# GpSimd's side work in an attention loop: four short pieces a quarter, and second pieces in units 3 to 24

## The chip, the cores and the metric

The kernel runs on one core of a Trainium2 chip. The core has five engines that each take their own instructions in order: TensorE (PE in the profile, with its weight loads as PEld), VectorE (DVE), ScalarE (ACT), GpSimd (POOL) and SyncE (SP, which here only issues transfers). They wait for each other by semaphores. The metric is the device time of one execution in microseconds (us), the median of several runs; lower is better.

## What is computed

One layer of a diffusion backbone on 1024 latent tokens of width 1024, with 256 context tokens, all in float32. The part that the change touches is the windowed attention:

```
hx = modulate(rmsnorm(x), sh1, sc1)
q, k, v, u, b, c, g_attn, g_conv = split(hx @ w_in)
for each block of 128 queries, each head:          # 8 blocks, 16 heads in 4 groups of 4
    s = q_block @ [k in the window of 384 keys | k_ctx of 256 keys].T / 8
    p = softmax([s masked | sink of the head])      # the sink only adds to the denominator
    o = p[:, :-1] @ [v in the window | v_ctx]
x = x + g1 * merge(o, conv(u, b, c), g_attn, g_conv) @ w_out
x = x + g2 * expert_choice_moe(modulate(rmsnorm(x), sh2, sc2))   # 16 experts of 128 tokens
return rmsnorm(x) * final_norm_g
```

A product of float32 matrices is made of three products of a high part and a low part (hi x hi, hi x lo, lo x hi). Large products behind the attention use a scheme of seven block products in place of eight, which wants sums and differences of the blocks of its operands beforehand.

## The kernel before

The stages are: modulation and the projections of q, k, v; the attention loop (about 250 to 600 us of the trace); the block products of the convolution branch and of the projections; the routing; the experts.

**The attention loop** (lines 784 to 802) has 32 units, one for each group g of four heads and block i of 128 queries. Unit n does this, in up to six steps s:

- `cur.turn(s)`: TensorE transposes the probabilities of one chunk of 128 keys for four heads (line 670, into psT), ScalarE casts them to the high part `th` (line 673), VectorE subtracts for the low part `tl` (line 674).
- `nxt.scores(s)` for s below 4: the scores of one head of unit n+2, two units ahead: TensorE's four products (lines 646 and 647), VectorE's masked maximum (line 649), ScalarE's exponential with its sum (line 653).
- At s = 3, `nxt.normalise()`: VectorE adds the sink's part to the sums (lines 660 and 662) and takes the reciprocal (line 663), then GpSimd multiplies the four heads' probabilities by it (line 665, four instructions). The transposes of unit n+2 need these.
- `pour(1)`: one step of the gate projection on TensorE (lines 40 to 44, three products into psF). These steps fill TensorE's time; there are 256 of them in all, and what is left of them is done behind the loop.
- `next(pool_left)` at some steps: one piece of GpSimd's side work, below.
- `cur.values(s - 1)`: the products with v (lines 682 and 683, into psB), at the last chunk ScalarE's copy and VectorE's sum (lines 687 and 688) and the store of the unit's result to `od`.

**GpSimd's side work** is a generator, `pool_work`, cut into pieces by its `yield`s:

- Three rows of the modulation (`mod_row`), each of eight pieces k = 0 to 7, with a piece ahead of the first row that only loads. A piece multiplies a loaded tile of 128 x 1024 by a column (line 477), adds it to `acc` (line 481; not for k = 0) and issues the load of the tile two pieces later (line 468, two tiles `w` in turn). At k = 1 it issues the loads for k = 2 and k = 3 together.
- `x_sums` for four quarters: sums and differences of the blocks of the layer's normalised input, in three parts of three, three and four instructions on 128 x 512 (line 696), in two tiles `w`. Behind the last part ScalarE casts each tile to `whi` (line 716), VectorE subtracts for `wlo` (line 717), and SyncE stores both to `xd`. The next quarter's first two parts write the same two tiles, so they wait for line 717.
- `o_sums` for two of four slices of the attention's output, heads of groups 0 and 2: the loads from `od` (line 738), four subtractions (line 725), then ScalarE's cast (line 728), VectorE's subtraction (line 729) and the stores to `sums`.

**What sets the order.** GpSimd's order in the loop is that of the code, since line 782 sets it by hand; it takes each instruction as soon as the one ahead is done and its waits are over. The other engines' orders come from the framework's scheduler, which places instructions by its own model; on chip they are fixed. Their order moves a little when the pieces move. A piece is taken at s = 4 of each unit, and at s = 1 where the condition of line 797 says so (second pieces). An assertion keeps the loads from `od` behind unit 24, as unit 23 is the last one of group 2.

Of the kernel before, what the change touches and what calls it, by code (L numbers as in the profile page):

```python
# [27 lines left out]
def hybrid_layer(ctx, tc, x, c, cx, c_ctx, w_mod, b_mod, norm1_g, w_in, attn_sink, conv_w,  # L28
# [320 lines left out]
    def pour(n):  # L349
        for _ in range(n):  # L350
            next(fill, None)
# [340 lines left out]
    def x_sums(ks):  # L692

        def part(hl, kh, th):
            return X[hl, kh, th].bitcast(F32)[:, ks]
        add, sub = ((lambda o, a, b, op=op: nc.gpsimd.tensor_tensor(out=o, in0=a, in1=b, op=op)) for op in (OP.add, OP.subtract))
        r = [w_tile(), w_tile()]
        t1, t2, t3, t4 = r[0][:, 0:512], r[0][:, 512:1024], r[1][:, 0:512], r[1][:, 512:1024]
        sub(t1, part(0, 0, 1), part(0, 0, 0))
        sub(t2, part(1, 0, 1), part(1, 0, 0))  # L700
        add(t1, t1, t2)
        yield
        sub(t3, part(0, 1, 1), part(0, 0, 1))
        sub(t4, part(1, 1, 1), part(1, 0, 1))
        add(t3, t3, t4)
        yield
        sub(t2, part(0, 1, 1), t1)
        add(t2, t2, part(1, 1, 1))
        sub(t4, part(0, 1, 0), t2)
        add(t4, t4, part(1, 1, 0))  # L710
        yield
        for n in range(2):
            hi = stage.tile([128, 2, 512], FR, name="whi", bufs=2)
            lo = stage.tile([128, 2, 512], FR, name="wlo", bufs=2)
            rv = r[n].rearrange("p (a b) -> p a b", a=2)
            nc.scalar.copy(out=hi, in_=rv)
            nc.vector.tensor_tensor(out=lo, in0=rv, in1=hi.bitcast(F32), op=OP.subtract)
            for hl, v in ((0, hi), (1, lo)):
                nc.sync.dma_start(out=xd[n * 2:n * 2 + 2, hl, :, ks].rearrange("n p f -> p n f"), in_=v.bitcast(F32))
# [23 lines left out]
    def w_tile():  # L743
        return osp.tile([128, 1024], F32, name="w", bufs=2)

    def pool_work():
        for n in range(1, 4):
            yield from mod_row(n, w_tile, lambda: osp.tile([128, 1024], F32, name="acc"), n < 3)
        for ks in range(4):
            yield from x_sums(ks)  # L750
        for ks in range(2):

            yield from o_sums(ks)
# [13 lines left out]
    piece = [0]  # L767
# [16 lines left out]
    for n in range(len(order)):  # L784
        cur = units.pop(0)
        nxt = Unit(*order[n + 2]) if n + 2 < len(order) else None
        units.append(nxt)
        nch = len(cur.chunks)
        for s in range(nch + 1):
            if s < nch:  # L790
                cur.turn(s)
            if nxt and s < 4:
                nxt.scores(s)
                if s == 3:
                    nxt.normalise()
            pour(1)
            if s == 4 or s == 1 and n % 3 == 0:
                piece[0] += 1
                assert piece[0] < 37 or n > 24
                next(pool_left, None)  # L800
            if s > 0:
                cur.values(s - 1)
# [240 lines left out]
    for m in range(4):  # L1043
        n = 3 * m + 3
# [872 lines left out]
```

## Time and profile before

| | us |
|---|---|
| three runs, median | 1795.31 |
| three runs, lowest and highest | 1794.01 and 1802.44 |
| the profiled execution | 1792.85 |
| its span, first to last instruction | 1791.0 |
| TensorE busy | 1711.4 (96%) |
| VectorE busy | 1412.4 (79%) |
| ScalarE busy | 1005.0 (56%) |
| GpSimd busy | 483.3 (27%) |

TensorE is busy in nearly all of the span, so a row of the profile matters where it ends one of TensorE's waits. GpSimd's 27% is an average over stages: it is at work most of the time from about 280 to 600 us, and hardly at all in many other stretches. Where an engine is followed in order of time, the bracket at a row's end is the idle time of that engine just before, and what ended it.

### The profile page before, as it was taken

What the parts mean: (1) busy time and instruction counts of PE and PEld (TensorE: products, weight loads), DVE (VectorE), ACT (ScalarE), POOL (GpSimd) and SP (SyncE); (2) the same over time, 40 slices, a digit from 0 to 9 for tenths busy, and PEclk for the clock granted to TensorE, in tenths of its full rate; (3) what the DMA queues carried; (4) which work ended last, traced back from release to release, by engine and by line L of the source; (5) the groups of instructions that cost most, each with busy time, mean ns of one, the idle gap of its engine ahead of it and who ended that gap; (6) DMA issues with size and microseconds to landing.
All of it is one profiled execution on the core that took longest, in us unless ns stands there. A gap on an engine that the chain in (4) does not pass through costs nothing.

```text
span 1791.0 us, 24156 instructions
## 1 busy us (share of the span) xinstructions
PE 1711.4 (96%) x8421; PEld 1377.7 (77%) x8421; DVE 1412.4 (79%) x2052; ACT 1005.0 (56%) x1448; POOL 483.3 (27%) x374
## 2 busy tenths in 40 slices
PE   8999999999999999999898999949999999999997
PEld 5777887888877787778676877837888888888874
DVE  6867568877778358766877775679999999999996
ACT  6642157667766323232434343327878878777874
POOL 0034027778678100000000003340042233224001
PEclk8999999999999999999999999969999999999999
DMA  9465364555345853333848354689999999999755
GB/s 349 134 200 187 115 238 141 181 164 165 101 131 178 311 172 119 110 115 106 305 132 293 105 213 181 247 319 335 368 398 384 398 396 382 395 397 397 292 200 200
DMA packets 210613, 427.75 MB, mean 239 GB/s; under 512 B 17512, under 2 KB 106920, under 8 KB 207420
## 3 DMA queue, kind: packets, MB, share of 16 engines
q1 hardware_dynamic: 176348, 359.30, 54.9%
q0 software_dynamic: 12544, 46.47, 8.5%
q10 hardware_dynamic: 21600, 20.45, 3.2%
q8 instruction: 66, 1.08, 0.2%
q14 instruction: 55, 0.45, 0.1%
HBM read 349.60 MB, written 76.56 MB: 238 GB/s over the span
## 4 chain that ended last, share of the span: by engine, by line
PE 82%; DVE 9%; DMA 3%; POOL 2%; issue 2%; ACT 2%; SPq 0%; POOLq 0%; ACTq 0%; DVEq 0%
PE psA L1722 20%; PE w L855 9%; PE psB L1722 5%; PE psF L1722 5%; PE psT L855 5%; PE psA L1288 4%; PE psT L670 3%; PE psA L402 2%; PE psF L855 2%; PE psA L400 2%; PE psA L401 2%; PE psF L40 2%; PE psF L44 2%; PE psF L42 2%; PE psB L683 2%
## 5 line engine op out<-in xcount | busy, mean ns | idle before, releaser
L1722 PE MATMUL psA<-part,xeh 128*128 128x512 f32 x1024 | 281.8, 392 | 0.5 <-ACT xeh L1710 0.5
L1722 PEld LDWEIGHTS psA<-part,xeh 128*128 128x128 f32 x1024 | 191.3, 188 | 39.9 <-ACT xeh L1710 1.0
L1757 POOL DMA_INDIRECT md<-ye,idxs x15 | 106.7, 7116 | 213.1 <-DVE ye L1754 213.1
L1722 PE MATMUL psA<-part,xel 128*128 128x512 f32 x512 | 163.2, 390 | 0.0
L1580 DVE TENSOR_TENSOR part<-er,part 128x1024 fp32r<-128x1024 f32 x118 | 138.4, 1219 | 5.4 <-ACT part L1578 2.0
L1578 ACT CAST part<-er 128x1024 fp32r<-128x1024 f32 x118 | 123.7, 1056 | 32.9 <-PE psA L1722 19.9
L649 DVE CUSTOM_DVE_ANT_0 p<-psA,msk,nsink 128x640 f32<-128x640 f32 (+1 forms) x128 | 107.7, 843 | 27.3 <-PE psA L647 25.7
L1410 POOL MEMSET onesb<- 128x128 bf16 x1 | 0.2, 204 | 464.2 <-issue 464.2
L674 DVE TENSOR_TENSOR tl<-psT,th 128x512 fp32r<-128x512 f32 x152 | 103.5, 685 | 21.8 <-ACT th L673 20.4
L665 POOL TENSOR_SCALAR p<-p,l 128x640 f32<-128x640 f32 (+1 forms) x128 | 101.6, 809 | 58.0 <-DVE l L663 14.7
L653 ACT ACTIVATE p<-p,nm 128x640 f32<-128x640 f32 (+1 forms) x128 | 103.0, 805 | 21.6 <-DVE nm L649 20.8
L867 ACT CAST whi<-raw 128x1024 fp32r<-128x1024 f32 x40 | 42.0, 1050 | 130.2 <-DVE raw L898 81.7
L673 ACT CAST th<-psT 128x512 fp32r<-128x512 f32 x152 | 88.0, 584 | 48.0 <-PE psT L670 47.0
L1722 PEld LDWEIGHTS psA<-part,xel 128*128 128x128 f32 x512 | 96.2, 188 | 20.5 <-DVE xel L1711 0.3
L1580 DVE TENSOR_TENSOR part<-mh,part 128x1024 fp32r<-128x1024 f32 x88 | 105.1, 1219 | 5.1 <-ACT part L1578 2.4
L1580 DVE TENSOR_TENSOR part<-ml,part 128x1024 fp32r<-128x1024 f32 x88 | 105.3, 1219 | 4.4 <-ACT part L1578 1.6
L1578 ACT CAST part<-ml 128x1024 fp32r<-128x1024 f32 x88 | 92.3, 1053 | 25.9 <-PE psA L1722 17.5
L1578 ACT CAST part<-mh 128x1024 fp32r<-128x1024 f32 x88 | 92.2, 1053 | 25.1 <-PE psA L1722 16.5
L1580 DVE TENSOR_TENSOR part<-mp,part 128x1024 fp32r<-128x1024 f32 x85 | 100.8, 1219 | 6.5 <-ACT part L1578 3.6
L1578 ACT CAST part<-mp 128x1024 fp32r<-128x1024 f32 x88 | 92.0, 1053 | 24.3 <-PE psA L1722 15.9
L1722 PE MATMUL psB<-part,hhh 128*128 128x512 f32 x256 | 98.6, 396 | 0.2 <-ACT hhh L1710 0.2
L670 PE MATMUL psT<-identr,p 128*128 128x128 f32 x608 | 94.2, 274 | 3.1 <-POOL p L665 2.9
(496 smaller groups left out, 4558.7 us busy)
## 6 DMA issues: line engine op xcount, KB each, us to landing
raw<-in_w_in_dram SPq DMA_DIRECT2D x49, 512.0 KB, 3.7
er<-in_w_exp_down_dram SPq DMA_DIRECT2D x47, 512.0 KB, 9.3
er<-in_w_exp_up_dram SPq DMA_DIRECT2D x38, 512.0 KB, 5.4
mp<-in_w_exp_gate_dram SPq DMA_DIRECT2D x36, 512.0 KB, 8.7
mh<-in_w_exp_up_dram SPq DMA_DIRECT2D x33, 512.0 KB, 5.7
ml<-in_w_exp_up_dram SPq DMA_DIRECT2D x33, 512.0 KB, 6.2
er<-in_w_exp_gate_dram SPq DMA_DIRECT2D x32, 512.0 KB, 8.0
mh<-in_w_exp_gate_dram SPq DMA_DIRECT2D x29, 512.0 KB, 7.7
```

The lines of the kernel that those rows point to most:

```text
L649: nc.vector.tensor_tensor_reduce(out=p, in0=sp[:, 512 - n:768], in1=msk.rearrange("p a b -> p (a b)")[:, mo * 128:mo * 128 + n + L], op0=O ...
L653: nc.scalar.activation(out=p, in_=p, func=AF.Exp, scale=-1.0, bias=self.nm4[:, h:h + 1], accum_out=self.l4[:, h:h + 1])
L665: nc.gpsimd.tensor_scalar(self.pr[h], self.pr[h], l4[:, h:h + 1], 1.0, op0=OP.mult, op1=OP.mult)
L670: nc.tensor.transpose(pt[:, h * 128:(h + 1) * 128], self.pr[h][:, ci * 128:(ci + 1) * 128], ident)
L673: nc.scalar.copy(out=th, in_=pt)
L674: nc.vector.tensor_tensor(out=tl, in0=pt, in1=th.bitcast(F32), op=OP.subtract)
L855: nc.tensor.matmul(ps_, lhsT=w[a][:, o + k], rhs=xs[b][:, k], start=(first and k + a + b == 0), stop=(k == 3 and a == 1), skip_group_check ...
L1288: nc.tensor.matmul(pa[:, s], lhsT=a[t // 2][k // 4][:, k % 4, ts], rhs=w[k][:, s], start=(j == 0 and a is mh and w is woh), stop=(j == NK ...
L1578: nc.scalar.copy(out=hi, in_=raw)
L1580: eng.tensor_tensor(out=lo, in0=raw, in1=hi.bitcast(F32), op=OP.subtract)
L1722: nc.tensor.matmul(outs[s], lhsT=lh[:, k], rhs=wt[:, s * 512:s * 512 + 512], start=(k == 0 and n == 0), stop=(k == NK - 1 and n == 2))
L1757: nc.gpsimd.indirect_dma_start(out=md, out_offset=bass.IndirectOffsetOnAxis(ap=idxs[:, e:e + 1], axis=0), in_=ye, in_offset=None, compute_ ...
```

## The change

Two places of the loop's side work change. In `x_sums` a `yield` is put between the two halves of the third part, so a quarter has four parts, of three, three, two and two instructions. The condition for second pieces, which was "at s = 1 in every third unit", becomes "at s = 1 in two of three units, from unit 3 to unit 24".

```diff
         sub(t2, part(0, 1, 1), t1)
         add(t2, t2, part(1, 1, 1))
+        yield
         sub(t4, part(0, 1, 0), t2)
         add(t4, t4, part(1, 1, 0))
         yield
...
-            if s == 4 or s == 1 and n % 3 == 0:
+            if s == 4 or s == 1 and n % 3 != 2 and 2 < n < 25:
                 piece[0] += 1
-                assert piece[0] < 37 or n > 24
+                assert piece[0] < 42 or n > 24
                 next(pool_left, None)
```

The pieces to be done go from 42 to 46 (the last of each count has nothing of GpSimd's in it). Second pieces stood in units 0, 3, 6 and so on to 30, eleven in all; now there are fifteen, in units 3, 4, 6, 7 and so on to 24, so units 0 to 2 and 25 to 31 have one piece each. Lines behind 708 move down by one in the changed kernel.

GpSimd's queue around units 3 and 4, first as it is, from the second piece of unit 3 on; the names with l_ are the reciprocals of one unit, so each row of line 665 is the normalise of one unit (5, then 6):

```order
L477 TENSOR_SCALAR w<-w,sf 128x1024
L481 TENSOR_TENSOR acc<-w,acc 128x1024
L468 DMA w<-in_w_mod_dram 128x1024
L665 TENSOR_SCALAR p<-p,l_2679 128x640 x4
L477 TENSOR_SCALAR w<-w,sf 128x1024
L481 TENSOR_TENSOR acc<-w,acc 128x1024
L468 DMA w<-in_w_mod_dram 128x1024
L665 TENSOR_SCALAR p<-p,l_2810 128x640 x4
```

The same place in the changed kernel, GpSimd's queue from the second piece of unit 3 (k = 2 of the first row) to the normalise of unit 6:

```order
L477 TENSOR_SCALAR w<-w,sf 128x1024
L481 TENSOR_TENSOR acc<-w,acc 128x1024
L468 DMA w<-in_w_mod_dram 128x1024
L665 TENSOR_SCALAR p<-p,l_2675 128x640 x4
L477 TENSOR_SCALAR w<-w,sf 128x1024
L481 TENSOR_TENSOR acc<-w,acc 128x1024
L468 DMA w<-in_w_mod_dram 128x1024
L477 TENSOR_SCALAR w<-w,sf 128x1024
L481 TENSOR_TENSOR acc<-w,acc 128x1024
L468 DMA w<-in_w_mod_dram 128x1024
L665 TENSOR_SCALAR p<-p,l_2806 128x640 x4
```

Between the normalises of units 5 and 6 there are two pieces in place of one. The piece just ahead of these rows is k = 1 in the changed kernel, which issues the load for the piece at their head; before it was k = 2.

GpSimd's queue around units 24 to 26, before: the normalise of unit 26, the four instructions that end the third quarter, the normalise of unit 27, the first part of the fourth quarter, the normalise of unit 28.

```order
L665 TENSOR_SCALAR p<-p,l_5448 128x640 x4
L696 TENSOR_TENSOR w<-x_754,w 128x512
L696 TENSOR_TENSOR w<-w,x_755 128x512
L696 TENSOR_TENSOR w<-x_518,w 128x512
L696 TENSOR_TENSOR w<-w,x_519 128x512
L665 TENSOR_SCALAR p<-p,l_5564 128x640 x4
L696 TENSOR_TENSOR w<-x_698,x_306 128x512
L696 TENSOR_TENSOR w<-x_699,x_307 128x512
L696 TENSOR_TENSOR w<-w 128x512
L665 TENSOR_SCALAR p<-p,l_5708 128x640 x4
```

The same place in the changed kernel, GpSimd's queue from the normalise of unit 26 to the first loads of `o_sums`:

```order
L665 TENSOR_SCALAR p<-p,l_5472 128x640 x4
L696 TENSOR_TENSOR w<-x_754,w 128x512
L696 TENSOR_TENSOR w<-w,x_755 128x512
L665 TENSOR_SCALAR p<-p,l_5586 128x640 x4
L696 TENSOR_TENSOR w<-x_518,w 128x512
L696 TENSOR_TENSOR w<-w,x_519 128x512
L665 TENSOR_SCALAR p<-p,l_5715 128x640 x4
L739 DMA acc<-od 128x1024
L739 DMA w<-od 128x1024
```

Ahead of the normalise of unit 27 there are two instructions in place of four, and the fourth quarter is over ahead of the normalise of unit 28. In both kernels the two parts just ahead of unit 26's normalise are the first two parts of a quarter, of the third before and of the fourth now.

ScalarE's queue in the last two units, before, up to the gate's last copies; line 728 is the cast of the attention's sums, 673 that of the probabilities:

```order
L673 CAST th<-psT 128x512 x3
L728 CAST whi<-acc 128x1024
L338 COPY gs<-psF 128x512
L673 CAST th<-psT 128x512 x2
L687 COPY ot<-psB 64x512
L673 CAST th<-psT 128x512 x2
L728 CAST whi<-acc 128x1024
L673 CAST th<-psT 128x512 x2
L338 COPY gs<-psF 128x512
L687 COPY ot<-psB 64x512
```

ScalarE's queue in the same two units of the changed kernel, where line 729 is that cast:

```order
L673 CAST th<-psT 128x512 x3
L729 CAST whi<-acc 128x1024
L338 COPY gs<-psF 128x512
L673 CAST th<-psT 128x512 x2
L214 CAST whi<-raw 128x1024
L687 COPY ot<-psB 64x512
L673 CAST th<-psT 128x512 x4
L338 COPY gs<-psF 128x512
L687 COPY ot<-psB 64x512
```

The cast in unit 30 is now the second one (the first stands in unit 28), and none is left in unit 31. In TensorE's queue two groups of gate products into psF (six products) now stand between the last value product and the first gate products into psB; before, the products into psB stood right behind it.

## Rows read from the trace of the kernel before

**Rows 1.** TensorE's waits, 250 to 605 us: us in total, times, longest

```profile
PE psB L683 <- DVE tl L674: 6.2, 9, 1.0
PE psT L670 <- POOL p L665: 2.9, 3, 1.9
PE psB L682 <- ACT th L673: 2.5, 2, 1.9
PE psB L40 <- DVE ot L688: 1.4, 1, 1.4
PE psB L682 <- DVE ot L688: 1.1, 1, 1.1
```

**Rows 2.** Stretches: us, busy of PE, PEld, DVE, ACT, POOL, clock, DMA

```profile
278.00:420.00 142.00, 136.86 (x791) 115.57 (x790) 113.05 (x222) 94.96 (x205) 110.97 (x108) 1.00 0.53 167
...
520.00:545.00 25.00, 22.01 (x117) 18.11 (x116) 19.13 (x36) 15.78 (x34) 23.03 (x20) 0.93 0.55 197
...
592.00:605.00 13.00, 8.96 (x29) 6.03 (x28) 4.43 (x5) 4.13 (x6) 5.72 (x4) 0.74 0.58 199
```

**Rows 3.** GpSimd in order of time, units 4 to 7: start, us, instruction, idle before

```profile
281.11 3.13 POOL L665 TENSOR_SCALAR p<-p,l 128x640 f32<-128x640 f32 x4 [1.36 <-DVE l L663]
284.22 1.13 POOL L477 TENSOR_SCALAR w<-w,sf 128x1024 f32<-128x1024 f32 x1
...
293.31 3.11 POOL L665 TENSOR_SCALAR p<-p,l 128x640 f32<-128x640 f32 x4
...
297.60 2.40 POOL L481 TENSOR_TENSOR acc<-w,acc 128x1024 f32<-128x1024 f32 x1
300.29 0.60 POOL L468 DMA_DIRECT2D w<-in_w_mod_dram  x1 [0.30 <-POOL acc L481]
...
312.10 2.69 POOL L665 TENSOR_SCALAR p<-p,l 128x512 f32<-128x512 f32 x4 [3.40 <-DVE l L663]
```

**Rows 4.** TensorE in order of time, first transposes of units 5 and 6

```profile
300.68 0.50 PE L683 MATMUL psB<-tl,v2t 128*128 128x512 f32 x1 [0.85 <-DVE tl L674]
301.02 0.60 PE L670 MATMUL psT<-identr,p 128*128 128x128 f32 x4
...
312.01 0.60 PE L670 MATMUL psT<-identr,p 128*128 128x128 f32 x4
```

**Rows 5.** VectorE in order of time, two instructions with two tiles read

```profile
297.78 2.24 DVE L660 TENSOR_TENSOR es<-sink,nm 128x4 f32<-128x4 f32 x1
...
493.16 1.22 DVE L717 TENSOR_TENSOR wlo<-w,whi 128x1024 fp32r<-128x1024 f32 x1
```

**Rows 6.** GpSimd's groups of instructions: times, busy us, mean ns, idle before

```profile
L696 POOL TENSOR_TENSOR w<-x,x 128x512 f32<-128x512 f32 x16 | 20.3, 1289 | 14.9 <-DVE wlo L717 14.9
```

**Rows 7.** Line 468, GpSimd's loads of the modulation's weights

```profile
DMA to landing us min/median/max: 3.8/4.8/10.5
```

**Rows 8.** GpSimd in order of time, normalises of units 23 and 26

```profile
493.20 3.76 POOL L665 TENSOR_SCALAR p<-p,l 128x512 f32<-128x512 f32 x4
...
520.13 2.55 POOL L696 TENSOR_TENSOR w<-x,x 128x512 f32<-128x512 f32 x2 [7.15 <-DVE wlo L717]
...
529.36 3.12 POOL L665 TENSOR_SCALAR p<-p,l 128x640 f32<-128x640 f32 x4
```

**Rows 9.** TensorE in order of time, transposes of units 26 and 27

```profile
530.21 0.48 PE L670 MATMUL psT<-identr,p 128*128 128x128 f32 x1 [1.93 <-POOL p L665]
...
542.93 0.33 PE L670 MATMUL psT<-identr,p 128*128 128x128 f32 x1 [0.72 <-POOL p L665]
```

**Rows 10.** ScalarE in order of time, its two casts of sums that waited

```profile
557.32 1.05 ACT L716 CAST whi<-w 128x1024 fp32r<-128x1024 f32 x1 [2.76 <-POOL w L696]
...
594.47 1.05 ACT L728 CAST whi<-acc 128x1024 fp32r<-128x1024 f32 x1 [3.62 <-POOL acc L725]
```

**Rows 11.** TensorE in order of time, the last unit's end

```profile
596.05 0.50 PE L682 MATMUL psB<-th,v2t 128*128 128x512 f32 x1 [1.92 <-ACT th L673]
...
600.89 0.79 PE L40 MATMUL psB<-x,whi 128*128 128x512 f32 x1 [1.39 <-DVE ot L688]
```

## The prediction

> **What bounds the kernel now.** I read the profile from the engine that is never idle for long. TensorE is busy nearly throughout, so the change can only move the time by the moments of the attention loop in which TensorE waits or runs at its lower clock. The first view is therefore who TensorE waited for from 250 to 605 us [rows 1]: five rows, 6.2 + 2.9 + 2.5 + 1.4 + 1.1 = 14.1 us, and only 2.9 us of it names GpSimd directly. The second view says where: 142 - 136.86 = 5.1 us between 278 and 420, 25 - 22.01 = 3.0 us between 520 and 545, and 13 - 8.96 = 4.0 us between 592 and 605, where the granted clock is 0.74 as well [rows 2]. The clock has two levels, 1.2 and 2.4 GHz; a mean of 0.74 over 13 us costs 13 x 0.26 = 3.4 us. No more than about 20 us are at stake, 1% of the kernel, and nothing behind 605 us is touched by the change.
>
> Then I followed each of these waits to its cause. GpSimd works strictly in its written order: normalise four heads of unit n+2, a piece, perhaps a second piece, normalise unit n+3. One normalise is 3.12 us, a long piece is a multiply of 1.13, an add of 2.40 and the issue of a load of 0.60, with the gaps 4.5 us [rows 3]. At 312.10 it has waited 3.40 us for VectorE's reciprocal (line 663), so with one piece a unit it is ahead [rows 3]; its normalise of unit 5 ends at 296.4, and the transposes that need it stand at 301.02, 4.6 us later [rows 3, 4].
>
> **Three waits of TensorE hang on GpSimd indirectly.** (a) Early: VectorE's tiny sum of line 660 took 2.24 us from 297.78 on, and ended with GpSimd's add of 297.60 to 300.00; the next subtraction came late and TensorE stood 0.85 us [rows 3 to 5]. (b) Units 26 and 27: GpSimd stood 7.15 us until the splitting of the previous quarter's sums freed their buffer, normalised unit 26 only from 529.36 on, and TensorE waited 1.93 us; unit 27 then cost 0.72 us [rows 8, 9]. (c) ScalarE's cast of a sum stood 2.76 us for GpSimd at 557 and 3.62 us at 594, with the casts of the probabilities queued behind it; TensorE's 1.92 us at 596 and 1.39 us at 601 follow the second [rows 10, 11].
>
> **The change, part by part.** GpSimd's work is the same: the same multiplies, adds, subtractions and loads. What moves is when.
>
> *Unit 27.* Ahead of its normalise stood four subtractions and additions of 1.29 us [rows 6]; now two stand there. It comes 2 x 1.3 = 2.6 us earlier, more than the 0.72 us by which it was late: gain 0.7 us. Unit 26 keeps its order (the first two parts of a quarter, behind a buffer wait that ends at the same place of ScalarE's and VectorE's order), so its 1.93 us and the clock of 0.93 in that window [rows 2] stay: 0.
>
> *Units 28 and 29.* The fourth quarter is finished with unit 25's piece, two units earlier than now, so ScalarE's 2.76 us wait goes. Of TensorE's waits it took 1.1 us (line 682 behind VectorE's line 688) and 2.5 - 1.92 = 0.6 us (line 682 behind line 673) [rows 1, 10, 11]: gain 1.7 us. What is late next is the first cast of the attention sums, which ScalarE now reaches in unit 28; GpSimd's four subtractions stand one unit ahead of it, and I charge 0.4 us for it.
>
> *The end.* The second cast of the attention sums moves from unit 31's place to unit 30's, and the loads for its subtractions from behind the last normalise to ahead of it; the last casts of the probabilities have nothing of GpSimd's ahead of them. That removes 4.0 us of idle time and, if TensorE keeps its pace, the 3.4 us of the low clock [rows 2]. Two groups of gate products now stand between the last value product and the switch to the other bank, which covers the 1.39 us [rows 11]; the first of them needs ScalarE's copy of the bank, for which I charge 0.4 us.
>
> Sum of the gains: 0.7 + 1.7 + 4.0 + 3.4 = 9.8, less 0.8 charged: 9.0 us.
>
> *The early units, lateness.* Now the cost. The second piece comes in units 3 and 4, 6 and 7 and so on. In unit 2 GpSimd ends the normalise of unit 4 at 284.2, then the piece that adds for the first time and issues two loads (1.13 + 2.40 + 2 x 0.6 + gaps 0.4 = 5.1 us, to 289.3), and the next piece, straight behind it, needs the first of these two loads: issued at 288.1, landed 4.8 us later in the median (3.8 to 10.5) [rows 7], so it starts at 292.9 and ends at 297.4. Queued behind this wait is the normalise of unit 5, to 300.5, against transposes at 301.02: 0.5 us to spare in place of 4.6. Two pieces more, to 309.5, and the normalise of unit 6, to 312.6, against 312.01 + 0.35 for its fourth transpose [rows 4]: 0.3 us late. From there GpSimd needs 3 x 3.12 + 5 x 4.5 = 31.9 us for three units that take 312.10 - 281.11 = 31.0 us [rows 3], but each of the two row changes has a piece without an add, 3.4 us shorter, so it catches up by unit 10. Loss 0.3 us; with the landing of 10.5 us it would be 6.0, with 3.8 none. I take 0.3, since the median is the nearest.
>
> *The early units, collisions.* Case (a) becomes likelier, because GpSimd is at work when lines 660 and 662 come. Between 278 and 420 TensorE lost 5.1 us, with five second pieces in the stretch (units 3, 6, 9, 12, 15); now there are nine (3, 4, 6, 7, 9, 10, 12, 13, 15). By second pieces the loss is 5.1 x 9/5 = 9.2, 4.1 us more; by the number of long adds, which is unchanged, it is 0 more. I take the middle, 2.0. The rule for it is in the Trainium skill, SBUF — State Buffer, section "Who interferes with whom": a VectorE instruction with two inputs in SBUF contends with a GpSimd instruction that reads SBUF, and whichever issues first holds the read side for the whole instruction. The trace agrees: line 660 reads two SBUF tiles and ended with the add. It speaks against this change in both directions: GpSimd's normalise at 493.20 took 3.76 us for four heads of 512, against 2.69 at 312.10, while VectorE's line 717 ran [rows 3, 5, 8].
>
> *The middle.* The second quarter's first two parts now both stand ahead of the normalise of unit 21, behind the same buffer wait as in (b), but one unit earlier against the transposes: 0. Ahead of unit 24 one more pair of 2.6 us stands, which the 2.6 us shorter stretch ahead of unit 25 gives back: 0 to 1 us, taken as 0.
>
> Net: 9.0 - 0.3 - 2.0 = 6.7 us gained. The profiled execution took 1792.85 us with a span of 1791.0, 2.5 us under the median of 1795.31; the difference is carried over: 1795.3 - 6.7 = **1788.6 us** (profiled execution 1786.2).
>
> **Rivals.** *The dense stretch tips over (slower).* From unit 5 to 16 GpSimd runs at its limit. If in each of these 12 units two of its instructions are stretched by 3.76 - 2.69 = 1.07 us [rows 3, 8], it needs 12 x 2.14 + 4 x 0.9 = 29.3 us more than there are; the spare 4.6 and the two short pieces, 6.8, leave 17.9 us of waiting, with 4.1 for collisions: 17.9 + 4.1 - 9.0 = 13 us slower, 1808. It decides from about 1.1 us a unit on (12 x 1.1 + 3.6 - 11.4 + 4.1 = 9.5). For it: the demand of 31.9 against 31.0. Against it: the normalises at 281, 293 and 529 show none of this stretch [rows 3, 8].
>
> *Every unit collides.* If GpSimd is in an add whenever line 660 or 662 comes, each of the 13 units from 4 to 16 pays what 300.68 paid, 13 x 0.85 = 11.1 in place of 5.1: 6 more instead of 2.0, net 2.7 gained, 1792.6. For it: GpSimd never waits there any more. Against: adds fill under half of its time.
>
> *The end doesn't close.* ScalarE waits for the sums in unit 30 as it did in unit 31, or the low clock comes anyway: 7.4 - 0.4 us fall away, 1795.6, no change. For it: those subtractions stand behind the normalise of unit 31, close ahead of the cast. Against: nothing but the cast's own 1 us stands behind it, and ScalarE had idle moments around it.
>
> *Unit 26 is helped too.* If GpSimd is a little later and the buffer is free when it arrives, the 1.93 us and 25 x 0.07 = 1.75 us of clock go as well: 1785.
>
> **How the numbers follow.** Forecast 0.54; end doesn't close 0.15; every unit collides 0.17; unit 26 too 0.08; tips over 0.06. The range reaches from 1782 (all gains of 9.8 and unit 26's 3.7) to 1797 (the end open, or the long landing, with the upper price of collisions); it leaves out the tipping and some of the spread of runs. A measurement of this kernel tells about 0.5% (9 us) from no change. Faster by over that needs nearly all the gains: a quarter of the forecast's chance and most of unit 26's, and some for costs that I set too high: 0.25. Slower by over that: the tipping, 0.07. Within: 0.68.
>
> **What would show it.** After: ScalarE's waits for GpSimd at lines 717 and 729 gone or under 1 us; no low clock around 595; TensorE's wait for GpSimd in unit 27 gone, in unit 26 still there; units 5 and 6 normalised within 1 us of their transposes, and TensorE's loss between 278 and 420 near 7 us. The forecast is wrong if that loss is over 12 us, or if the stretch from 590 on still loses 4 us.

## The result and the profile after

The changed kernel takes 1817.15 us in the median (1816.61 to 1817.78) beside 1798.07 us for the kernel before on the same chip: ratio 1.0115, 95% interval 1.0094 to 1.0136. It is slower by some 20 us, where 6.7 us of gain were forecast. The profiled execution took 1816.61 us with a span of 1814.4, 23.8 us over the one of before.

Set side by side by the same instruction of TensorE, the two traces part early. Of the 608 transposes of line 670 the first comes 1.2 us earlier than before, the 100th (at 301 us) 0.7 us earlier, the 200th 5.0 us later, the 300th 12.7, the 400th (472 before, 489 now) 17.2. From there to the 480th half a microsecond is added. Unit 26 adds 2.6 (the 500th is 20.3 us late), units 27 to 29 give back 3.6 (the 540th is 16.7 late), and the end takes as much again: the first block product behind the attention (631 before) is 20.5 us late. So the early units, and what follows them up to the 400th transpose, cost some 18 us, unit 26 nearly 3, and what lies behind it, which was to give 9, gives nothing. The last 3 us are a net sum: 1 us is regained between 880 and 1060 us and 4 us are lost behind 1200, where nothing was changed; no cause of them was looked for.

TensorE's waits from 250 to 650 us, after (us in total, times, longest), answering [rows 1]:

```profile
PE psB L683 <- DVE tl L674: 14.1, 8, 3.8
PE psB L682 <- DVE ot L688: 4.9, 2, 2.8
PE psT L670 <- POOL p L665: 4.1, 3, 3.5
PE psF L40 <- ACT gs L338: 2.8, 2, 2.6
```

The first row has grown from 6.2 to 14.1 us: TensorE waits for VectorE's residue of the probabilities (the low part `tl` of line 674). For GpSimd it waits 3.5 us at unit 26 and hardly anywhere else. The stretches, after (us, busy of PE, PEld, DVE, ACT, POOL, granted clock, DMA), answering [rows 2]:

```profile
278.00:420.00 142.00, 129.01 (x712) 108.34 (x711) 111.54 (x198) 86.36 (x186) 117.68 (x109) 0.95 0.53 166
420.00:520.00 100.00, 97.56 (x554) 82.94 (x553) 78.94 (x157) 68.75 (x145) 74.44 (x67) 0.98 0.41 129
...
545.00:570.00 25.00, 21.08 (x109) 17.75 (x109) 14.71 (x29) 12.68 (x26) 18.67 (x19) 0.86 0.26 78
570.00:592.00 22.00, 18.82 (x105) 15.22 (x103) 18.37 (x33) 14.65 (x29) 14.90 (x15) 1.00 0.61 215
592.00:605.00 13.00, 12.19 (x62) 10.33 (x63) 7.45 (x15) 7.63 (x18) 4.29 (x6) 0.87 0.46 144
605.00:625.00 20.00, 16.95 (x78) 12.95 (x77) 8.60 (x12) 8.21 (x13) 4.39 (x3) 0.91 0.43 143
```

Between 278 and 420 TensorE idles 142 - 129.01 = 13.0 us (5.1 before), and the clock of 0.95 costs at most 142 x 0.05 = 7.1 us (nothing before). From 420 to 520 it idles 2.4 us (0.3 before) and the clock costs 2.0. The increases add up to 7.9 + 7.1 + 2.1 + 2.0 = 19.1 us, a little more than the 18.4 us between the first transpose and the 400th, since some 1 us of the low clock fell into idle time (0.85 from 310 to 314, below).

**Where VectorE was.** VectorE and GpSimd in order of time, after (start, us, instruction):

```profile
295.97 3.39 DVE L660 TENSOR_TENSOR es<-sink,nm 128x4 f32<-128x4 f32 x1
...
306.89 5.68 DVE L215 TENSOR_TENSOR wlo<-raw,whi 128x1024 fp32r<-128x1024 f32 x1 [0.26 <-ACT whi L214]
...
374.06 5.40 DVE L215 TENSOR_TENSOR wlo<-raw,whi 128x1024 fp32r<-128x1024 f32 x1
```

```profile
306.65 0.59 POOL L468 DMA_DIRECT2D w<-in_w_mod_dram  x1 [0.30 <-DVE tl L674]
307.29 3.12 POOL L665 TENSOR_SCALAR p<-p,l 128x640 f32<-128x640 f32 x4
310.39 1.11 POOL L477 TENSOR_SCALAR w<-w,sf 128x1024 f32<-128x1024 f32 x1
311.58 3.21 POOL L481 TENSOR_TENSOR acc<-w,acc 128x1024 f32<-128x1024 f32 x1
```

An instruction is called held here when it stands in the trace far longer than it takes by itself. Line 215, the subtraction that splits the gate's weights, takes 1.2 us undisturbed; in the kernel before its longest up to 450 us was 1.90. Here it takes 5.68 us. GpSimd runs five instructions on end meanwhile, a normalise of four heads and a row piece's multiply; the add behind them has to wait for that multiply, and between 311.50 and 311.58 GpSimd stands still. The subtraction ends at 312.57, 1.07 us after that pause began. At 374 it is the same: the multiply ends at 378.39, the subtraction at 379.46. The sum of four columns at 295.97 ends at 299.36, where the multiply of 298.24 ends. TensorE's waits for the residue that follow are 2.00 us (to 300.01), 3.81 (to 313.90) and 3.51 (to 380.93). Behind the 3.81 us the granted clock falls (stretches of the kernel after, same columns as above):

```profile
310.00:314.00 4.00, 0.19 (x2) 0.10 (x1) 4.00 (x5) 0.72 (x3) 3.92 (x3) 0.85 1.04 402
314.00:319.60 5.60, 5.60 (x17) 4.54 (x18) 3.55 (x7) 1.93 (x5) 5.09 (x7) 0.50 0.50 168
```

After a stretch in which it had stood nearly all of 4 us, TensorE works on at 0.50, which is 1.2 GHz, to 319.6. The clock is 0.50 as well from 381.1 to 384.4, behind the 3.51 us, and from 411.9 to 415.1, behind a wait of 1.81 us; behind the 2.00 us at 300.01 it stays at 1.00.

**Where the end went.** ScalarE in order of time, and SyncE's queue, after:

```profile
591.10 1.04 ACT L214 CAST whi<-raw 128x1024 fp32r<-128x1024 f32 x1 [2.82 <-DMA sums<-whi]
...
613.74 1.04 ACT L214 CAST whi<-raw 128x1024 fp32r<-128x1024 f32 x1 [4.26 <-DMA sums<-whi]
```

```profile
586.32 0.36 SPq L735 DMA_DIRECT2D sums<-w  x1
586.77 1.46 SPq L735 DMA_DIRECT2D sums<-whi  x1
```

The waits of ScalarE for GpSimd of [rows 10] are gone, as forecast. But the cast of the gate's weights now needs a `whi` buffer (there are two, shared by lines 214, 717 and 729) that the sum's cast of 582.65 has just filled, and the store that frees it stands in SyncE's queue behind the store of the other sum, from `w`. That one waits for GpSimd's last subtraction (`SPq L735 <- POOL w L726`, 11.0 us in two waits). TensorE's waits of 2.61 us at 592.81 and 2.79 us at 616.25 follow.

**Unit 26.** GpSimd and TensorE in order of time, after, answering [rows 8, 9]:

```profile
547.18 4.72 POOL L665 TENSOR_SCALAR p<-p,l 128x640 f32<-128x640 f32 x4
```

```profile
549.64 0.48 PE L670 MATMUL psT<-identr,p 128*128 128x128 f32 x1 [3.53 <-POOL p L665]
```

The normalise of unit 26 is still behind the wait for the buffer, and now takes 4.72 us in place of 3.12: its first head lasts to 549.58, since line 215 took its turn in the midst of it (547.71, 1.21 us). The wait is 3.53 us in place of 1.93, and the clock from 545 to 570 is 0.86.

### The profile page after: what moved, and what is told of

The parts are those of the page before. It is cut to its first block, busy times and chain, and to the rows that moved or that the text cites. A ratio compares the mean times of both kernels' runs of the same rounds, so it can differ in the third digit from the quotient of the medians.

```text
span 1814.4 us, 24158 instructions
## 1 busy us (share of the span) xinstructions
PE 1724.6 (95%) x8421; PEld 1391.0 (77%) x8421; DVE 1419.5 (78%) x2052; ACT 1004.5 (55%) x1448; POOL 484.1 (27%) x374
## 3 DMA queue, kind: packets, MB, share of 16 engines
q8 instruction: 66, 1.08, 0.2%
## 4 chain that ended last, share of the span: by engine, by line
PE 56%; DVE 6%; DMA 2%; issue 1%; ACT 1%; POOL 0%; SPq 0%; POOLq 0%; ACTq 0%; DVEq 0%
PE psA L1723 19%; PE w L856 9%; PE psB L1723 5%; PE psF L1723 5%; PE psT L856 4%; PE psA L1289 4%; PE psF L856 2%; PE psT L1708 2%; PE psB L856 1%; DMA x<-yd 1%; DVE rsc L1595 1%; PE part L1482 1%; DVE x L1029 1%; DVE q L934 1%; DVE mp L941 0%
## 5 line engine op out<-in xcount | busy, mean ns | idle before, releaser
L1723 PEld LDWEIGHTS psA<-part,xel 128*128 128x128 f32 x512 | 96.5, 189 | 20.5 <-DVE xel L1712 0.3
```

What stands on the lines that cost most here:

```text
L1723: nc.tensor.matmul(outs[s], lhsT=lh[:, k], rhs=wt[:, s * 512:s * 512 + 512], start=(k == 0 and n == 0), stop=(k == NK - 1 and n == 2))
```

## The experiments

Theory S (a string of GpSimd's instructions without a pause holds VectorE; from e5 on, as theory P, that VectorE gets in only at GpSimd's pauses) and theory Q (the store in SyncE's queue) stand against rival L (GpSimd comes too late with its normalises) and a loss from the fourth short piece. Where an edit adds a line to the normalise, line numbers behind it are 1 to 3 higher.

**e1_early_old**, which units carry the early loss:

```
-if s == 4 or s == 1 and n % 3 != 2 and 2 < n < 25:
+if s == 4 or s == 1 and (n % 3 == 0 if n < 16 or n > 24 else n % 3 != 2):
```

> The changed kernel, with second pieces as before up to unit 15 and after unit 24 (every third unit) and the new rule only in units 16 to 24; the four short pieces a quarter stay. Theory S (the loss is made where GpSimd's pieces stand close together in units 3 to 15, by VectorE instructions that cannot start while GpSimd's instructions follow each other without a pause): the 13.0 us that TensorE idles between 278 and 420 go back to 5 to 6, the granted clock there to 1.00, and the time is that of the kernel before plus the 3 us that the end costs: ratio 1.000 to 1.003, about 1800 us. Rival L (the loss comes from the shorter pieces or from the order after unit 16): the ratio stays at 1.008 or more, 1812 us or more.

Measured: ratio 1.0073 (1.0049 to 1.0097). Between 278 and 420 the loss is gone: TensorE is busy 137.49 of 142 us at a clock of 1.00, and the 300th transposes 1.6 us earlier than before. The time missed the expectation of 1.000 to 1.003: three pieces fewer are done by unit 24, and the sums come late again; ScalarE, in order of time:

```profile
499.50 1.04 ACT L717 CAST whi<-w 128x1024 fp32r<-128x1024 f32 x1 [5.28 <-POOL w L696]
...
607.67 1.05 ACT L729 CAST whi<-acc 128x1024 fp32r<-128x1024 f32 x1 [7.70 <-POOL acc L726]
```

The early loss belongs to the second pieces of units 3 to 15. The pieces that they bring forward are needed at the end.

**e2_rule_only**, the kernel before with the new rule alone:

```
-if s == 4 or s == 1 and n % 3 == 0:
+if s == 4 or s == 1 and n % 3 != 2 and 2 < n < 22:
```

> The kernel before with the new rule for second pieces alone (two of three units, from the 3rd to the 21st, 43 pieces), and three pieces a quarter as before. Theory S: the early loss is all there, TensorE idles 11 to 14 us between 278 and 420 with VectorE blocked for over 3 us at least three times; the end is reached with the sums two or three units earlier than before. Ratio 1.008 to 1.012, 1812 to 1819 us. Rival (the fourth short piece makes the loss): ratio within 1.003.

Measured: ratio 1.0113 (1.0075 to 1.0150). Line 215 takes 5.69 us at 307.57 and 5.40 at 374.75, and TensorE's waits between 278 and 420 are led by

```profile
PE psB L683 <- DVE tl L674: 13.2, 7, 3.8
```

The fourth short piece is not needed for the early loss: it comes with the rule alone. What that piece does by itself was not tried.

**e3_gap**, a write behind each head of a normalise:

```
 nc.gpsimd.tensor_scalar(self.pr[h], self.pr[h], l4[:, h:h + 1], ...)
+nc.gpsimd.memset(gap, 0.0)
```

> The changed kernel, and behind each of the four multiplies of a normalise on GpSimd a write of one column to a tile that nothing reads, some 0.1 us in which GpSimd reads no SBUF tile. Theory S (VectorE's instruction with two SBUF inputs waits for a whole string of GpSimd instructions that follow each other, not for one): no VectorE instruction between 278 and 420 is held for over 2.5 us any more (it was 5.7 and 5.4), TensorE's idle time there falls from 13.0 to 6 to 9 us with fewer stretches at 1.2 GHz, ratio 1.003 to 1.007, about 1807 us. Rival L (GpSimd is at its limit, and its normalises come late): GpSimd has some 0.4 us a unit more to do, the ratio is 1.0115 or more, 1817 us or more. Third possibility: the pause does not let VectorE in, the blocks of over 5 us stay and so does the time.

Measured: ratio 1.0130 (1.0092 to 1.0167); the third possibility. GpSimd and VectorE in order of time:

```profile
310.13 0.79 POOL L666 TENSOR_SCALAR p<-p,l 128x640 f32<-128x640 f32 x1
310.88 0.09 POOL L667 MEMSET gap<- 128x1 f32 x1
310.95 0.79 POOL L666 TENSOR_SCALAR p<-p,l 128x640 f32<-128x640 f32 x1
```

```profile
310.22 4.54 DVE L216 TENSOR_TENSOR wlo<-raw,whi 128x1024 fp32r<-128x1024 f32 x1
```

The write starts while the multiply still runs, and the next multiply starts while the write runs: GpSimd never stands still, and VectorE is held until the multiply of the row piece ends at 313.69 (1.07 us before 314.76). So it isn't enough that GpSimd does something else for a moment.

**e4_o2_queue**, the second sum's store on GpSimd's own queue:

```
-sums_out(0, ks, 1, o2)
+nc.gpsimd.dma_start(out=sums[0][2:4, 0, :, ks].rearrange("n p f -> p n f"), in_=o2)
```

> The changed kernel, with the store of the second attention sum (from w) issued by GpSimd itself behind its last subtraction instead of by SyncE. Theory Q (the end gains nothing since ScalarE's cast of the gate weights needs a whi buffer whose store stands in SyncE's queue behind that store, which waits for GpSimd): ScalarE's waits of 2.8 and 4.3 us at 591 and 613.7 for sums<-whi fall under 0.5 us, TensorE's 2.6 and 2.8 us behind them go with the stretches at 1.2 GHz at 592.7 and 616.6: 5 to 8 us less than the changed kernel, 1809 to 1812 us, ratio 1.006 to 1.009. Rival: ScalarE waits there for something else that comes as late (the load of the next gate block, a VectorE subtraction), and the time stays within 2 us of 1817.

Measured: ratio 1.0066 (1.0045 to 1.0087). ScalarE's wait for `sums<-whi` is 0.3 us in place of 7.1, TensorE has no wait over 0.3 us from 592 to 650, and from 592 to 625 the clock is 1.00. Theory Q holds. The times fall in two groups, 1797.5 and 1798.4, and eight from 1806 to 1810, and the profiled execution is of the first. Its early units are told by one meeting:

```profile
307.10 1.23 DVE L215 TENSOR_TENSOR wlo<-raw,whi 128x1024 fp32r<-128x1024 f32 x1 [0.26 <-ACT whi L214]
```

```profile
307.52 3.80 POOL L665 TENSOR_SCALAR p<-p,l 128x640 f32<-128x640 f32 x4
```

Up to here the instructions are those of the changed kernel. There the subtraction started 0.40 us ahead of the normalise and was held for all of it; here it starts 0.42 us ahead, takes 1.23 us, and the normalise pays 0.68. Without the two long holds of line 215 TensorE idles 7.5 us between 278 and 420 in place of 13.0, at a clock of 1.00, and the 300th transpose is 2.1 us later than before instead of 12.7. That is what the long holds cost: some 10 us. The two groups lie as far apart, but one trace was kept, so that the eight slower executions had the long holds is not shown.

**e5_pause**, in place of the write an instruction that needs the multiply's result:

```
+nc.gpsimd.tensor_scalar(gap, self.pr[h][:, 0:1], 1.0, 1.0, op0=OP.mult, op1=OP.mult)
```

> The changed kernel, and behind each of the four multiplies of a normalise on GpSimd one more instruction, of one column, that reads what the multiply has just written. It cannot start before the multiply has ended, as an add of a row piece cannot start before its own multiply; there the trace shows 0.08 us between the two, and there the held VectorE instructions got in (at 311.5, 378.4 and 299.4 us of the changed kernel), and in e3_gap too, where the writes followed without a pause. Theory P (VectorE gets in only where GpSimd stands still between two instructions): no VectorE instruction between 278 and 420 is held for over 2.5 us (the length of a long add), the idle time of TensorE there falls from 13.0 to 7 or 8 us, its stretches at 1.2 GHz there go, 9 to 11 us less than the changed kernel, ratio 1.004 to 1.007. Rival L (GpSimd is at its limit): 0.7 us more of GpSimd's time a unit make the normalises late, ratio 1.0115 or more. Rival R (who gets in hangs on something else): blocks of over 5 us stay, ratio 1.011.

Measured: ratio 1.0103 (1.0079 to 1.0127). GpSimd now pauses behind every head, and TensorE's waits from 250 to 650 are

```profile
PE psT L672 <- POOL p L666: 15.6, 23, 3.5
...
PE psB L685 <- DVE tl L676: 1.6, 3, 1.0
```

The waits for VectorE's residue fall from 14.1 to 1.6 us. Line 215 takes 3.24 us at most (2.5 were expected), behind one long add (404.39 to 406.79), and ends 1.08 us after it. TensorE idles 6.8 us between 278 and 420 (7 or 8 were expected), at a clock of 0.98. So with a pause behind every head the holds of over 5 us are gone, as theory P says (that VectorE gets in only at a pause is too strong: see the last section). Rival L is right on the price: a head takes 1.05 us with its pause in place of 0.78, 1.1 us a unit and not 0.7, and GpSimd's normalises come late 23 times.

**e6_o2_u26**, e4's edit and the second piece of unit 24 in unit 26:

```
+if s == 4 or s == 1 and (n % 3 != 2 and 2 < n < 24 or n == 26):
```

> The changed kernel with the store of the second attention sum on GpSimd's queue (as e4_o2_queue), and the second piece of unit 24 moved to unit 26, so that unit 26's normalise no longer stands behind the subtraction that waits for a free buffer. Theory: TensorE's 3.5 us wait for unit 26 goes with the 6.8 us at 1.2 GHz behind it: 5 to 7 us less than e4_o2_queue in the same mode of the early units, ratio 1.001 to 1.004, with some runs 10 us lower. Rival: the wait moves to unit 27, whose normalise now has the same buffer wait one unit ahead: ratio 1.006 as e4_o2_queue.

Measured: ratio 1.0013 (0.9987 to 1.0039). TensorE's 3.5 us wait for unit 26 is 0.45 us, and the clock from 520 to 605 is 1.00. This execution has the long holds (5.68 and 5.41 us) and took 1803.8; others of the kernel lie down to 1785.4. The ratio is in the range expected. In the two traces, from 520 to 570, TensorE idles 3.9 us at a clock that costs 3.5 in e4 and idles 0.9 at 1.00 here, a gain of 6.4 us.

**e7_pause_o2_u26** and **e8_halves**, e6 with the four pauses, and then with row pieces in halves as well:

```
+for hs in (slice(0, 512), slice(512, 1024)):
+    nc.gpsimd.tensor_scalar(w[:, hs], w[:, hs], sf[:, 0, k:k + 1], 1.0, op0=OP.mult, op1=OP.mult)
+    if k:
+        nc.gpsimd.tensor_tensor(out=acc[:, hs], in0=w[:, hs], in1=(first if k == 1 else acc)[:, hs], op=OP.add)
```

> The edits of e5_pause and e6_o2_u26 together. If the three losses are separate (held VectorE instructions, ScalarE behind the store, unit 26), their gains add up: 1817 - 10 - 8 - 6 = 1793 us on the scale on which the kernel before takes 1798, ratio 0.995 to 0.999. If the clock takes back what one of them gives, 1.000 to 1.003.

> The edits of e7_pause_o2_u26, and each row piece worked in two halves of 512 columns: multiply, add, multiply, add, each add behind the pause that its own multiply makes, so that the longest string without a pause is 1.2 + 0.6 us and not 2.4. Theory P: the 1.6 to 2.4 us for which lines 660 and 662 are still held shrink to under 1.9, TensorE's idle time between 278 and 420 falls under 6 us, 1 to 3 us less than e7_pause_o2_u26, ratio 0.993 to 0.998. Rival: the two more instructions a piece, some 0.2 us, and the clock take it back: the same as e7_pause_o2_u26.

Measured: 1.0019 (1.0001 to 1.0037) and 1.0081 (1.0062 to 1.0101); for e8 neither expectation holds. The gains don't add up where GpSimd pays: TensorE waits 9.6 us for its normalises in e7 (19 times) and 20.7 us in e8 (34 times), against 1.0 in e6. In e8 the waits for VectorE's residue are down to 2.4 us and the time is worse all the same. The time of e7 is the one named for the case that the clock takes gains back, but by rival L's waits and not by the clock (1.00 from 420 to 640, 0.98 from 278 to 420).

**e10_one_pause**, e6 with a pause behind the first head only, and **e11_every_other**, e6 with second pieces in units 0, 2, ... 22 and in 17, 21 and 26:

> e6_o2_u26 with one pause a normalise, behind its first head, in place of the four of e7_pause_o2_u26. Theory P with a price for the pause: an instruction of VectorE that meets the normalise at its start is held for 0.8 + 1.1 us and some in place of 5.4 to 5.7, and GpSimd pays about 0.27 us a unit in place of 1.1, so that its normalises stay ahead of the transposes (waits of TensorE for GpSimd in 250 to 650 under 4 us, where four pauses made 9.6 to 15.6): 5 to 9 us less than e6_o2_u26 where its early blocks came, ratio 0.995 to 0.999. Rival: an instruction that comes later in the string is held as long as before, and the time is that of e6_o2_u26, 1.000 to 1.003.

> e6_o2_u26 with second pieces in every other unit (0, 2, ... 22) and in 17 and 21, the same number ahead of unit 24 as in e6_o2_u26. If the loss of the early units comes from GpSimd's instructions following each other for several units on end, it lies between that of every third unit (4.5 to 5.1 us idle in 278 to 420) and that of two in three (13.0): 6 to 9 us, ratio 0.997 to 1.001. If it comes from single meetings only, which any shift makes anew, it may be as low as 5 or as high as 13.

Measured: 0.9990 (0.9974 to 1.0006) and 0.9972 (0.9956 to 0.9987). One pause keeps TensorE's waits for GpSimd at 1.8 us, and no instruction of VectorE takes over 3.11 us between 278 and 450. Its interval overlaps that of e6 and holds 1, so by the time alone e10 is told from neither. In e11 TensorE idles 8.4 us between 278 and 420; both possibilities named allow that, so the run doesn't decide between them. One meeting in it is the plainest of all; VectorE and GpSimd in order of time:

```profile
286.98 4.51 DVE L662 TENSOR_TENSOR l<-l,es 128x4 f32<-128x4 f32 x1
```

```profile
287.27 3.11 POOL L665 TENSOR_SCALAR p<-p,l 128x640 f32<-128x640 f32 x4
290.36 1.11 POOL L477 TENSOR_SCALAR w<-w,sf 128x1024 f32<-128x1024 f32 x1
291.56 2.40 POOL L481 TENSOR_TENSOR acc<-w,acc 128x1024 f32<-128x1024 f32 x1
```

A sum of four columns takes 4.51 us, to the pause at 291.47.

**e9_early_old_late_new**, e4's edit, early second pieces as before, and one in every unit from 16 to 23 and in 26:

```
+if s == 4 or s == 1 and (n < 16 and n % 3 == 0 or 16 <= n < 24 or n == 26):
```

> e6_o2_u26 with second pieces up to unit 15 as before the change (every third unit), and in every unit from 16 to 23, so that as many pieces stand ahead of unit 24. If the two parts add up, early units as before (TensorE idles about 5 us between 278 and 420, no held instruction of over 2.5 us, as e1_early_old showed) and the end as in e6_o2_u26 (12 us won back between the 400th transposes and the first block product): 1786 to 1790 us where the kernel before takes 1796, ratio 0.994 to 0.997. Rival, as e1_early_old showed it: with the pieces late and dense, ScalarE's and VectorE's casts of the sums come before GpSimd has them, TensorE loses 8 us and more between 420 and 520, ratio 1.001 to 1.006.

Measured: 1789.39 us beside 1795.91, ratio 0.9956 (0.9941 to 0.9970). Both parts add up, though the rival's loss is there too at half its size (TensorE busy 95.75 of 100 us from 420 to 520). The rest, stretches of e9:

```profile
278.00:420.00 142.00, 136.80 (x790) 115.54 (x789) 113.05 (x222) 94.95 (x205) 110.95 (x108) 1.00 0.54 167
...
592.00:605.00 13.00, 12.79 (x60) 10.12 (x59) 3.53 (x6) 3.57 (x6) 0.00 (x0) 1.00 0.69 229
```

**e12_e9_halves**, e9 with the halves of e8 and no pause:

> e9_early_old_late_new, and each row piece worked in two halves of 512 columns (multiply, add, multiply, add), as in e8_halves, without the pauses in the normalises. Theory P: what still holds lines 660, 662 and 215 in e9 is the long add (1.5 to 2.4 us, eleven times between 276 and 435); a half add holds them for 1.3, and TensorE's idle time between 278 and 420 falls from 5.2 to under 4 us: 1 to 3 us less than e9, ratio 0.993 to 0.996. Rival L: GpSimd's halves take 0.4 us more a piece, its normalises come late in the units with a second piece as in e8_halves (20.7 us of waits for GpSimd), ratio 0.997 to 1.001.

Measured: 1784.80 us beside 1796.77, ratio 0.9935 (0.9917 to 0.9952). TensorE, 278 to 420:

```profile
278.00:420.00 142.00, 140.05 (x814) 119.11 (x813) 110.91 (x229) 97.08 (x209) 123.52 (x146) 1.00 0.57 174
```

It idles 1.95 us where the kernel before idles 5.1, and GpSimd's 12.6 us of further work are hidden, for with a second piece in every third unit it has room. Theory P's reason holds only in part: line 215 at 363.80 takes 3.82 us and a sum at 446.19 takes 3.80, more than any such instruction up to 450 us in e9 (2.39). This is faster than both kernels by more than the intervals; whether it beats e9 the two intervals don't tell, since they overlap.

## Why the prediction was wrong

*What bounds the kernel* and the places were right: all differences up to 640 us lie in TensorE's waits and its clock. The forecast named its own refutations. A loss over 12 us between 278 and 420: it is 13.0. A stretch from 590 on that still loses 4 us: from 592 to 625 TensorE idles 3.9 us, and the clock costs some 3.4 more.

*Early units, lateness* (0.3): right. The loads did hold GpSimd, and unit 5 is normalised only at 298.25, but 2.1 us ahead of its transposes; unit 6 is 6.2 us ahead, as TensorE itself had been delayed. (The sign named for it, within 1 us of the transposes, did not come.)

*Early units, collisions* (2.0, between 0 and 4.1): this step failed. Measured: 7.9 us of further idle time and 6 to 7 us of clock in that stretch, and 4 us more behind it, where one further sum is held (2.37 us at 442.33) and TensorE then stands 2.09 us. The step counted meetings. Its bound scaled the 5.1 us lost before by the number of second pieces, and its rival charged every unit 0.85 us, the price of a meeting with a single add [rows 4, 5]. The number of waits did not grow; their length did (TensorE's waits for the residue from 278 to 420, before and after):

```profile
PE psB L683 <- DVE tl L674: 5.1, 7, 1.0
```

```profile
PE psB L683 <- DVE tl L674: 12.6, 6, 3.8
```

The strings are not new: a normalise and the multiply behind it, five instructions, follow each other without a pause in both kernels. What moved is where they begin. Before, eight of the twelve normalises of units 4 to 15 start behind a wait of 0.2 us or more, for VectorE's reciprocal at 281.11 and 312.10 [rows 3]; now it is six. The two long holds of line 215 stand at the normalises of units 6 and 12, which had such a wait before (0.22 and 1.70 us) and now start right behind the issue of a load. That this is why line 215 is caught there is argued, not shown. And the clock was charged at the end alone, though it fell behind three waits of this stretch too.

The rule cited was the Trainium skill, SBUF — State Buffer, section "Who interferes with whom": the first to issue holds the read side for its whole instruction. The trace agrees on the pair of engines and differs on the length: line 215 was held over five instructions, though by the trace it had started 0.40 us ahead of them; the measurement decides.

*Unit 27* (0.7): right, it has no wait. *Unit 26* (0): it grew by 1.6 us of wait and some 1.7 us of clock; the stretch of GpSimd by VectorE, which the prediction cited against the change, happened there. *The middle* (0): two small waits for GpSimd, 0.2 and 0.3 us, and the sum held at 442.33, counted above.

*Units 28, 29 and the end* (9.1 with the clock, less 0.8): this step failed too. The waits named did go, and new ones of the same size came: 2.61 and 2.79 us with the clock at 0.87 and 0.91, so the end took back what units 27 to 29 had gained. The step looked at who ScalarE waits for, and not at the buffers that its casts fill: the cast moved one unit forward, and the one behind it needed a `whi` whose store was queued behind GpSimd. e4 shows it by undoing that alone. A row of the kernel before already had such a wait (ScalarE):

```profile
561.19 1.05 ACT L716 CAST whi<-w 128x1024 fp32r<-128x1024 f32 x1 [1.11 <-DMA xd<-whi]
```

Two terms of this sum were read too high as well. The 0.6 us of line 682 ended at 554.13, ahead of ScalarE's wait for the sum (554.56 to 557.32), so they did not come from it. And the 3.4 us of clock overlap the idle time: from 598.2 to 605.0 the clock was 0.50 with TensorE busy 5.41 of 6.80 us, which makes 2.7 us.

*The rivals.* "Tips over" gave the right side and, with 1808, about two thirds of the loss (13 of 19 us), but by the wrong mechanism: GpSimd was to be late. GpSimd did become the bound in e5, e7 and e8, where each unit got 1.1 us more of it. "The end doesn't close" happened, by another wait. "Every unit collides" came near the idle time (11.1 us, measured 13.0), but by many short meetings in place of few long ones.

Added up by ratios: moving the store is worth 8.8 us (1.0115 to 1.0066, of which some 2 us because two of its ten times lie 10 us lower), unit 26 9.5 (to 1.0013, of which the traces show 6.4 between 520 and 570), the new spacing of the second pieces 10.2 (to 0.9956). Each ratio is known to about 0.2%, some 4 us, so these are rough. What stays open: who wins a meeting. The same two instructions, 0.40 and 0.42 us apart, went either way.

## What to carry to other kernels

Bound the price of a meeting of VectorE and GpSimd by the longest run of GpSimd's instructions without a pause that can follow, not by one instruction, and look at what makes GpSimd pause. When a piece of work is moved forward, list the buffers that its instructions fill and the queue that each store stands in, since the next user of the buffer waits for the slowest store ahead. Work that fits a slack engine in the sum of its busy time may still not fit between its deadlines.

## What the runs showed of the hardware that was not expected

In the changed kernel five VectorE instructions with two inputs in SBUF took over 2 us between 278 and 450, and each ended at a pause of GpSimd of 0.08 us or more: the sums 0.02 to 0.03 us after the pause began, line 215 1.07 us after. Pauses of 0.04 to 0.05 us (between the issue of a load and the normalise) did not let line 215 in, in either of its two long holds. In e5 an instruction that needs the result of the one ahead starts 0.08 to 0.09 us after it has ended; in e3 an independent one starts before the one ahead has ended.

A pause is not always needed, though. In the kernel before, line 215 got its turn between the last head of a normalise and the multiply behind it, which follow without a pause, and the multiply took 2.08 us in place of 1.1 (VectorE, then GpSimd):

```profile
369.08 1.41 DVE L215 TENSOR_TENSOR wlo<-raw,whi 128x1024 fp32r<-128x1024 f32 x1
```

```profile
366.28 3.13 POOL L665 TENSOR_SCALAR p<-p,l 128x640 f32<-128x640 f32 x4 [1.70 <-PE psB L682]
369.40 2.08 POOL L477 TENSOR_SCALAR w<-w,sf 128x1024 f32<-128x1024 f32 x1
```

At 399.88 the same happens between two heads, and in the changed kernel behind 480 us several times; at 547.71 line 215 even takes its turn, by the trace, while a head is under way. So a pause ends a hold in these traces, and without one VectorE was sometimes let in at the next instruction and sometimes held over as many as five. What decides between the two is not shown.
